# Gate products of one-hot matrices: two products in a rounded format instead of one in plain fp32

## The chip, the cores and the metric

The kernel runs on one core of a Trainium2 chip. A core has a matrix engine (PE), whose weight loads the profile lists apart (PEld), and three engines for element-wise work: VectorE (DVE), ScalarE (ACT) and GpSimd (POOL). SyncE (SP) issues the transfers from the memory outside. Every engine works through its own queue in the order in which its instructions were written there; engines wait for each other by semaphores. The metric is the time of one execution in microseconds (us) on the device.

## The reference

The program is two small networks, one after the other, on 256 tokens of width 1024. The part that matters here is the retrieval of experts (`peer`) in the first. For each token and each of 8 heads it takes the 16 best scores against two sets of 128 keys, forms the 16 best pairs, and turns their scores into gates by a softmax. A pair (i1, i2) names one of 128 x 128 experts:

```python
idx = jnp.take_along_axis(cand_i, pos, axis=-1)          # i1 * 128 + i2
g = jax.nn.softmax(top_s, axis=-1)
act = jax.nn.gelu(jnp.einsum('thkd,td->thk', expert_u[idx], t).astype(jnp.float32))
return jnp.einsum('thk,thkd->td', (g * act).astype(t.dtype), expert_v[idx])
```

So each token has 8 x 16 = 128 slots, each with two indices and a gate. All arithmetic is fp32 in the reference.

## The kernel before

The kernel gathers nothing. It computes the activations of all 128 x 128 experts for all tokens, in a tile X of 128 partitions (i1) x 128 (i2) x 256 tokens, and multiplies them by a matrix of gates that is zero where a token did not choose an expert.

The weights of the whole program come as a stream of 128 x 1024 fp32 tiles ("raw", 4 buffers). Each is split into a high part in the rounded format ("wh": ACT copies it, L296) and a rest ("wl": DVE subtracts, L297), with 3 buffers each, because a product of fp32 accuracy is made of three products of rounded operands (high by high, low by high, high by low: L334 to L336). The rounded format is called fp32r in the profile; plain fp32 operands need no split. The stream is kept three tiles ahead: the split for step i2+3 is written as soon as the buffer of step i2 is free.

The gate stretch is the second part of the loop over i2 (128 steps), which makes the activations of the experts (., i2). A step has 24 products of 128 x 256 on PE into a tile "main". From step 56 on, 64 "gate groups" of four tokens are spread over 70 steps (64 of them hold one group, 6 none). A group makes, per token:

- "oh1" on POOL (L1138): in row "slot", a one where the column number equals the slot's first index;
- "oh2" on DVE (L1141): the same for the second index, times the slot's gate;
- one plain fp32 product oh1 by oh2 on PE (L1144) of 128 x 128 into a tile "aux", which is the token's gate matrix.

The tile's columns of later steps are copied into X by ACT (L1146); the steps already done are multiplied into X by DVE (L1147). Later steps' activations come through a small tile "ge" (gelu on ACT: L1203 for tokens without gates yet, straight into X; L1206 for the others) and are multiplied into X by DVE (L1207). oh1 and oh2 have 4 buffers each, so both are made some groups ahead.

A scheduler in the framework writes the order of every queue at build time. `slots` runs once for each half of the tokens just before the stretch: it transposes the slots' indices and gates, so that a token is a column, into slotT[0] to slotT[2].

Of the kernel before, what the change touches and what calls it, by code (L numbers as in the profile page):

```python
# [8 lines left out]
F32 = mybir.dt.float32  # L9
F32R = mybir.dt.float32r  # L10
U32 = mybir.dt.uint32
U8 = mybir.dt.uint8
AF = mybir.ActivationFunctionType
OP = mybir.AluOpType
# [29 lines left out]
OHB = 4  # L44
# [131 lines left out]
def build(tc, A, out):  # L176
    nc = tc.nc
    V, S, T, G = nc.vector, nc.scalar, nc.tensor, nc.gpsimd

    with ExitStack() as ctx:  # L180
# [8 lines left out]
        def PS():  # L189
            return psum.tile([128, 512], F32, tag="aux", name="aux")  # L190
# [7 lines left out]
        for name in W_IN_ORDER:  # L198
            n = W_IN_COLS[name][1]
# [118 lines left out]
        ident, iota, pair_rows = cst[:, 0:128], cst[:, 128:256], cst[:, 256:272]  # L318
# [141 lines left out]
        with ExitStack() as fctx:  # L460
# [77 lines left out]
            for e in range(2):  # L538
                c = slice(256 * e, 256 * e + 256)
# [116 lines left out]
            def colmajor(ap):  # L656
                return ap.rearrange("p (r w) -> p w r", w=64)
# [290 lines left out]
            def gate_ev(gain):  # L948
                def ev(f, ps):
                    if not gate:  # L950
# [8 lines left out]
                              for g in range(2)], gl_gen(), fm_gen(512, ev, 0, 1),  # L959
                            fm_gen(256, lambda f, ps: S.activation(out=gq[:, f, :].rearrange("p (w r) -> p w r", r=4),  # L960
                                                                   in_=colmajor(ps[:, 0:256]), func=AF.Copy, scale=0.125), 0, 2),
# [35 lines left out]
            for k in st1.end(eps1[:, 0:1], [xlat[:, k] for k in range(8)]):  # L997
                n, o, g, b = xlat[:, k], x1[:, k], vc("lng")[:, k:k + 1], bcen[:, k:k + 1]
# [8 lines left out]
            m2, r = tl("m2", [256], "b0"), tl("r2m", [256], "b1")  # L1007
# [4 lines left out]
            for k in range(8):  # L1012
                n = xlat[:, k]
# [4 lines left out]
                t = tl("tmod", [256], "Qt", 2)  # L1018
# [5 lines left out]
        with ExitStack() as ectx:  # L1024
# [4 lines left out]
            up = uctx.enter_context(tc.tile_pool(name="uphase", bufs=1))  # L1029
# [3 lines left out]
            def carve(shape, dt=F32):  # L1033
                n = int(np.prod(shape))
                o = carve_at[0]
                carve_at[0] += n
                assert carve_at[0] <= 128 * 256
                ap = flat[:, o:o + n]
                if dt is not F32:
                    ap = ap.bitcast(dt)  # L1040
                names = " ".join("abcd"[:len(shape)])
                return ap.rearrange(f"p ({names}) -> p {names}", **dict(zip("abcd", shape))) if len(shape) > 1 else ap
# [13 lines left out]
            tmp2 = carve([256])  # L1056
# [8 lines left out]
            e2 = carve([2, 8, 16])  # L1065
            ii2 = [[carve([8, 16]) for _ in range(2)] + [e2[:, t]] for t in range(2)]
            sm = carve([2, 8])
            slotT = [up.tile([128, 256], F32, name=f"slotT{j}") for j in range(3)]
            qT = [carve([256]) for _ in range(2)]

            def topk16(vals, idx, src, tmp):
# [53 lines left out]
            def slots(t, ii):  # L1125
                pt = PS()
                for j in range(3):
                    T.transpose(pt[:, 128 * j:128 * j + 128], ii[j].rearrange("p h k -> p (h k)"), ident)
                for j in range(3):
                    V.tensor_copy(slotT[j][:, 128 * t:128 * t + 128], pt[:, 128 * j:128 * j + 128])  # L1130

            def gate_group(tg, m):

                t0 = 4 * tg
                oh1 = up.tile([128, 4, 128], F32, name="oh1", tag="oh1", bufs=OHB)
                oh2 = up.tile([128, 4, 128], F32, name="oh2", tag="oh2", bufs=OHB)
                for j in range(4):
                    G.tensor_scalar(oh1[:, j], iota, slotT[0][:, t0 + j:t0 + j + 1], None, op0=OP.is_equal)  # L1138
                pg = PS()
                for j in range(4):  # L1140
                    V.tensor_scalar(oh2[:, j], iota, slotT[1][:, t0 + j:t0 + j + 1], slotT[2][:, t0 + j:t0 + j + 1],  # L1141
                                    op0=OP.is_equal, op1=OP.mult)
                for j in range(4):
                    T.matmul(pg[:, 128 * j:128 * j + 128], oh1[:, j], oh2[:, j], start=True, stop=True)  # L1144
                pgv = pg.rearrange("p (t i) -> p i t", t=4)
                S.activation(out=X[:, m:, t0:t0 + 4], in_=pgv[:, m:], func=AF.Copy)  # L1146
                V.tensor_tensor(X[:, 0:m, t0:t0 + 4], X[:, 0:m, t0:t0 + 4], pgv[:, 0:m], OP.mult)  # L1147
# [32 lines left out]
            for i2 in range(128):  # L1180
                hi, lo = W.get("s")
                p = PM()[:, 0:256]
                for k in range(8):
                    c = slice(128 * k, 128 * k + 128)
# [3 lines left out]
                if i2 < GATE_FROM:  # L1188
                    S.activation(out=X[:, i2, :], in_=p, func=GE)
                    credit += TOPK_RATE  # L1190
                    while (credit > 0 or i2 == GATE_FROM - 1) and not done_tk:
                        try:
                            credit -= next(tk)
                        except StopIteration:
                            done_tk = True
                    if i2 == GATE_FROM - 1:
                        slots(0, ii2[0])
                        slots(1, ii2[1])
                    continue

                t = 4 * done
# [7 lines left out]
                while done < upto:  # L1209
                    gate_group(done, i2 + 1)  # L1210
                    done += 1
# [45 lines left out]
            for i2 in range(125):  # L1257
                w = W.get("s")
                xsplit(i2 + 2)
                x = xs_t.pop(i2)  # L1260
# [530 lines left out]
```

## Time and profile before

| | us |
|---|---|
| median of 3 runs (least, most) | 2248.65 (2248.22, 2250.47) |
| the profiled execution's own time | 2249.63 |
| its span in the profile | 2247.6 |
| gate stretch, 541 to 792 us: PE busy | 251.00 |
| the same: DVE, POOL, ACT busy | 200.55, 207.12, 107.26 |

The span is from the first to the last profiled instruction. A busy time is the union of an engine's instructions. PE and the weight loads overlap, and products overlap each other, so one product's duration is longer than the distance from its start to that of the next; the distance is what a stream of them costs. The same holds, in a smaller measure, for ACT and DVE: an instruction starts a little before the one ahead of it ends. In a waits row, "A line <- B line" says that A sat idle until B's instruction.

### The profile page before, as it was taken

Reading aid. Unit: us, or ns where it says so; the run is one execution under the profiler, and the core shown is the slowest. Engines: PE = TensorE matmul, PEld = TensorE weight load, DVE = VectorE, ACT = ScalarE, POOL = GpSimd, SP = SyncE. Lnnn points to the kernel's source line nnn. Section 1 sums busy time; section 2 is a strip of 40 time slices with the busy share of each in tenths; the row PEclk is TensorE's granted clock in tenths of the full one; section 3 lists DMA queues with packets and bytes.
Section 4 is the critical chain, followed back from the end, with each engine's and each line's share of the span. In section 5 each row is a group of like instructions: output and inputs, shape, how many; then the busy total and the mean of one; then the engine's idle time right before and its main releaser. Section 6 shows DMA issues by size and latency. Waiting matters only on the chain.

```text
span 2247.6 us, 40177 instructions
## 1 busy us (share of the span) xinstructions
PE 2167.5 (96%) x15660; PEld 2034.8 (91%) x15660; DVE 1546.6 (69%) x2819; ACT 1174.9 (52%) x2036; POOL 391.6 (17%) x411
## 2 busy tenths in 40 slices
PE   7999889899999999999989998999999999899998
PEld 4988789899999988888879998899999999889998
DVE  6899879935778866666665556885566555878554
ACT  5755554444444354554554445675456444676443
POOL 0000031225978700000020003020001001302000
PEclk9999899999999999999999999999999999999999
DMA  7544244465444467666646563345564556334564
GB/s 278 160 160 132 85 124 151 160 193 173 143 147 145 141 210 246 197 192 195 202 151 187 171 189 112 100 135 174 174 189 145 173 171 195 103 104 138 185 181 126
DMA packets 101998, 367.37 MB, mean 163 GB/s; under 512 B 11440, under 2 KB 13360, under 8 KB 100528
## 3 DMA queue, kind: packets, MB, share of 16 engines
q1 hardware_dynamic: 101808, 364.81, 51.2%
q8 instruction: 122, 2.00, 0.4%
q14 instruction: 68, 0.56, 0.1%
HBM read 363.72 MB, written 1.05 MB: 162 GB/s over the span
## 4 chain that ended last, share of the span: by engine, by line
PE 79%; DVE 14%; ACT 3%; issue 3%; DMA 1%; POOL 1%; SPq 0%; DVEq 0%; POOLq 0%; ACTq 0%
PE main L336 19%; PE main L335 18%; PE main L334 18%; PE aux L1255 5%; PE aux L1254 5%; PE aux L1256 5%; DVE wl L297 3%; PE aux L1144 3%; DMA raw<-wa 1%; DVE X L1076 1%; DVE X L1074 1%; DVE SB L840 1%; DVE Qt L820 1%; DVE X L1073 0%; DVE X L1075 0%
## 5 line engine op out<-in xcount | busy, mean ns | idle before, releaser
L296 ACT ACTIVATE wh<-raw 128x1024 fp32r<-128x1024 f32 (+1 forms) x630 | 658.2, 1046 | 679.3 <-PE main L335 354.9
L297 DVE TENSOR_TENSOR wl<-raw,wh 128x1024 fp32r<-128x1024 f32 (+1 forms) x606 | 741.0, 1224 | 382.4 <-ACT wh L296 381.9
L336 PE MATMUL main<-hh,wl 128*128 128x256 f32 (+1 forms) x2808 | 807.0, 288 | 17.5 <-DVE wl L297 17.5
L334 PE MATMUL main<-hh,wh 128*128 128x256 f32 (+1 forms) x2808 | 811.8, 290 | 11.5 <-DVE hh L444 5.7
L335 PE MATMUL main<-hl,wh 128*128 128x256 f32 (+1 forms) x2808 | 805.4, 287 | 1.6 <-DVE hl L448 1.1
L336 PEld LDWEIGHTS main<-hh,wl 128*128 128x128 f32 x2808 | 535.2, 191 | 22.0 <-DVE wl L297 20.9
L334 PEld LDWEIGHTS main<-hh,wh 128*128 128x128 f32 x2808 | 534.1, 190 | 16.2 <-DVE hh L444 6.6
L335 PEld LDWEIGHTS main<-hl,wh 128*128 128x128 f32 x2808 | 533.8, 190 | 3.5 <-DVE hl L448 2.2
L396 POOL TENSOR_TENSOR acc<-acc,sqk 128x272 f32<-128x272 f32 (+1 forms) x29 | 37.3, 1286 | 1438.0 <-ACT sqk L389 1437.9
L1138 POOL TENSOR_SCALAR oh<-cst,slotT 128x128 f32<-128x128 f32 x256 | 209.3, 834 | 38.2 <-PE aux L1144 32.4
L334 PE MATMUL main<-ah,wh 128*128 128x272 f32 (+1 forms) x704 | 201.7, 286 | 0.0
L335 PE MATMUL main<-al,wh 128*128 128x272 f32 (+1 forms) x704 | 201.2, 286 | 0.0
L336 PE MATMUL main<-ah,wl 128*128 128x272 f32 (+1 forms) x704 | 200.6, 285 | 0.0
L1254 PE MATMUL aux<-wh,xsh 128*128 128x512 f32 x512 | 199.3, 390 | 0.0
L1255 PE MATMUL aux<-wl,xsh 128*128 128x512 f32 x512 | 199.3, 389 | 0.0
L1256 PE MATMUL aux<-wh,xsl 128*128 128x512 f32 x512 | 199.2, 389 | 0.0
L339 ACT ACTIVATE xsh<-X 128x256 fp32r<-128x256 f32 x128 | 53.4, 418 | 165.7 <-PE aux L1255 163.9
L336 PEld LDWEIGHTS main<-ah,wl 128*128 128x128 f32 x704 | 132.4, 188 | 0.0
L334 PEld LDWEIGHTS main<-ah,wh 128*128 128x128 f32 x704 | 132.3, 188 | 0.0
L335 PEld LDWEIGHTS main<-al,wh 128*128 128x128 f32 x704 | 132.2, 188 | 0.0
L1255 PEld LDWEIGHTS aux<-wl,xsh 128*128 128x128 f32 x512 | 96.1, 188 | 20.2 <-DVE wl L297 0.3
L1254 PEld LDWEIGHTS aux<-wh,xsh 128*128 128x128 f32 x512 | 96.0, 188 | 20.2 <-ACT wh L296 0.3
(507 smaller groups left out, 3126.7 us busy)
## 6 DMA issues: line engine op xcount, KB each, us to landing
raw<-uT SPq DMA_DIRECT2D x128, 512.0 KB, 3.6
raw<-pv SPq DMA_DIRECT2D x128, 512.0 KB, 4.2
raw<-ffn_gate SPq DMA_DIRECT2D x88, 512.0 KB, 3.6
raw<-ffn_up SPq DMA_DIRECT2D x88, 512.0 KB, 3.6
raw<-win SPq DMA_DIRECT2D x72, 512.0 KB, 4.0
raw<-ffn_down SPq DMA_DIRECT2D x64, 512.0 KB, 3.6
raw<-wa SPq DMA_DIRECT2D x32, 512.0 KB, 4.4
raw<-wout SPq DMA_DIRECT2D x24, 512.0 KB, 3.6
```

Source lines behind the costliest of these rows:

```text
L296: S.activation(out=hi[:, :n], in_=t[:, :n], func=AF.Copy)
L297: (G if mode == "p" else V).tensor_tensor(lo[:, :n], t[:, :n], hi[:, :n].bitcast(F32), OP.subtract)
L334: T.matmul(o, lh, rh, start=start, stop=False)
L335: T.matmul(o, lh, rl, start=False, stop=False)
L336: T.matmul(o, ll, rh, start=False, stop=stop)
L339: S.activation(out=hi, in_=src, func=AF.Copy)
L396: (G if self.k < (5 if self.pe == 7 else 2) else V).tensor_tensor(self.acc2, self.acc2, q, OP.add)
L1138: G.tensor_scalar(oh1[:, j], iota, slotT[0][:, t0 + j:t0 + j + 1], None, op0=OP.is_equal)
L1144: T.matmul(pg[:, 128 * j:128 * j + 128], oh1[:, j], oh2[:, j], start=True, stop=True)
L1254: T.matmul(y, x[0][:, c], w[0][:, f], start=(i2 == 0), stop=False)
L1255: T.matmul(y, x[0][:, c], w[1][:, f], start=False, stop=False)
L1256: T.matmul(y, x[1][:, c], w[0][:, f], start=False, stop=(i2 == 127))
```

## The change

Each gate is split into its rounded part and a rest. `slots` stores the rounded gates in slotT[2] (written by ACT in the rounded format, read back as fp32 under the name `rounded`) and in slotT[3] the ratio of the rest to the rounded part: a subtraction, a maximum with 1e-30, a reciprocal and a multiplication on DVE, for each half of the tokens.

In a group, oh1 and oh2 are written in the rounded format, oh2 with the rounded gate. A third tile, oh3, is oh2 times the slot's ratio, made by ACT, four instructions per group. PE makes two products per token, oh1 by oh2 and oh1 by oh3, added up in the same tile. The buffers of the one-hots go from 4 to 3 each.

```diff
-            slotT = [up.tile([128, 256], F32, name=f"slotT{j}") for j in range(3)]
+            slotT = [up.tile([128, 256], F32R if j == 2 else F32, name=f"slotT{j}") for j in range(4)]
+            rounded = slotT[2].bitcast(F32)
...
-                for j in range(3):
-                    V.tensor_copy(slotT[j][:, 128 * t:128 * t + 128], pt[:, 128 * j:128 * j + 128])
+                c = slice(128 * t, 128 * t + 128)
+                for j in range(2):
+                    V.tensor_copy(slotT[j][:, c], pt[:, 128 * j:128 * j + 128])
+                S.activation(out=slotT[2][:, c], in_=pt[:, 256:384], func=AF.Copy)
+                r = rounded[:, c]
+                V.tensor_tensor(slotT[3][:, c], pt[:, 256:384], r, OP.subtract)
+                rec = tmp2[:, 0:128]
+                V.tensor_scalar(rec, r, 1.0e-30, None, op0=OP.max)
+                V.reciprocal(out=rec, in_=rec)
+                V.tensor_tensor(slotT[3][:, c], slotT[3][:, c], rec, OP.mult)
...
-                oh1 = up.tile([128, 4, 128], F32, name="oh1", tag="oh1", bufs=OHB)
-                oh2 = up.tile([128, 4, 128], F32, name="oh2", tag="oh2", bufs=OHB)
+                oh1, oh2, oh3 = [up.tile([128, 4, 128], F32R, name=n, tag=n, bufs=3) for n in ("oh1", "oh2", "oh3")]
...
-                    V.tensor_scalar(oh2[:, j], iota, slotT[1][:, t0 + j:t0 + j + 1], slotT[2][:, t0 + j:t0 + j + 1],
+                    V.tensor_scalar(oh2[:, j], iota, slotT[1][:, t0 + j:t0 + j + 1], rounded[:, t0 + j:t0 + j + 1],
                                     op0=OP.is_equal, op1=OP.mult)
                 for j in range(4):
-                    T.matmul(pg[:, 128 * j:128 * j + 128], oh1[:, j], oh2[:, j], start=True, stop=True)
+                    S.activation(out=oh3[:, j], in_=oh2[:, j].bitcast(F32), func=AF.Copy, scale=slotT[3][:, t0 + j:t0 + j + 1])
+                for j in range(4):
+                    for x in (oh2, oh3):
+                        T.matmul(pg[:, 128 * j:128 * j + 128], oh1[:, j], x[:, j], start=(x is oh2), stop=(x is oh3))
```

The scheduler writes the queues anew. In the rows below a name's number tells the buffer's allocation: wh and wl with neighbouring numbers belong to one weight tile, oh2 and oh3 with neighbouring numbers to one group. Lines after the change: oh2 is L1150, oh3 L1153, the copy of "aux" L1158, its multiplication L1159, the gelus L1215 and L1218, the multiplication by "ge" L1219.

ACT's queue in the middle of the stretch, before the change, two steps:

```order
L1206 ACTIVATE ge_8122<-main_8096 128x184
L1146 ACTIVATE X_2900<-aux_8131 128x21x4
L296 ACTIVATE wh_8194<-raw_8146 128x1024
L1203 ACTIVATE X_2900<-main_8148 128x68
L1206 ACTIVATE ge_8174<-main_8148 128x188
L1146 ACTIVATE X_2900<-aux_8183 128x20x4
L296 ACTIVATE wh_8246<-raw_8198 128x1024
```

ACT's queue after the change, at the same step:

```order
L1158 ACTIVATE X_2900<-aux_8555 128x21x4
L1153 ACTIVATE oh3_8733<-oh2_8732,slotT3_2915 128x128 x4
L296 ACTIVATE wh_8635<-raw_8578 128x1024
L1215 ACTIVATE X_2900<-main_8580 128x68
L1218 ACTIVATE ge_8606<-main_8580 128x188
L1158 ACTIVATE X_2900<-aux_8616 128x20x4
L1153 ACTIVATE oh3_8794<-oh2_8793,slotT3_2915 128x128 x4
L296 ACTIVATE wh_8696<-raw_8639 128x1024
```

The four instructions of oh3 stand right ahead of the copy wh, and each reads an oh2.

DVE's queue at that step, before the change:

```order
L1147 TENSOR_TENSOR X_2900<-X_2900,aux_8131 128x107x4
L1141 TENSOR_SCALAR oh2_8334<-cst_72,slotT1_2913,slotT2_2914 128x128 x3
L1141 TENSOR_SCALAR oh2_8386<-cst_72,slotT1_2913,slotT2_2914 128x128
L297 TENSOR_TENSOR wl_8195<-raw_8146,wh_8194 128x1024
L1207 TENSOR_TENSOR X_2900<-X_2900,ge_8174 128x188
L1147 TENSOR_TENSOR X_2900<-X_2900,aux_8183 128x108x4
L1141 TENSOR_SCALAR oh2_8386<-cst_72,slotT1_2913,slotT2_2914 128x128 x3
L1141 TENSOR_SCALAR oh2_8438<-cst_72,slotT1_2913,slotT2_2914 128x128
L297 TENSOR_TENSOR wl_8247<-raw_8198,wh_8246 128x1024
```

DVE's queue after the change:

```order
L1159 TENSOR_TENSOR X_2900<-X_2900,aux_8555 128x107x4
L1150 TENSOR_SCALAR oh2_8732<-cst_72,slotT1_2913,slotT2_2914 128x128 x4
L297 TENSOR_TENSOR wl_8636<-raw_8578,wh_8635 128x1024
L1219 TENSOR_TENSOR X_2900<-X_2900,ge_8606 128x188
L1159 TENSOR_TENSOR X_2900<-X_2900,aux_8616 128x108x4
L1150 TENSOR_SCALAR oh2_8793<-cst_72,slotT1_2913,slotT2_2914 128x128 x4
L297 TENSOR_TENSOR wl_8697<-raw_8639,wh_8696 128x1024
```

All four oh2 of a group stand ahead of the subtraction wl, which reads the wh that ACT makes behind that group's oh3. PE's queue has, in both kernels, a group's products between the 24 of one step and the 24 of the next: 4 in plain fp32 before, 8 in the rounded format after. The 6 steps without a group lie alike.

## Rows read from the trace of the kernel before

**Rows 1.** The page, part 1, whole span: busy us, share, count of each engine.

```profile
PE 2167.5 (96%) x15660; PEld 2034.8 (91%) x15660; DVE 1546.6 (69%) x2819; ACT 1174.9 (52%) x2036; POOL 391.6 (17%) x411
```

**Rows 2.** Busy time of each engine in the gate stretch (first line names the columns).

```profile
core 0: us, PE busy (x) PEld busy (x) DVE busy (x) ACT busy (x) POOL busy (x), PEclk, DMA share, GB/s
541.00:792.00 251.00, 251.00 (x2151) 250.97 (x2150) 200.55 (x454) 107.26 (x268) 207.12 (x254) 1.00 0.46 145
```

**Rows 3.** Waits in that stretch: who for whom, us in total, times, longest.

```profile
ACT wh L296 <- PE main L335: 145.4, 69, 2.3
DVE oh L1141 <- PE aux L1144: 41.5, 57, 1.4
POOL oh L1138 <- PE aux L1144: 32.4, 49, 3.3
```

**Rows 4.** Timeline of PE, one step: start us, duration us, engine, line, op, tiles, shapes, count.

```profile
644.26 1.05 PE L1144 MATMUL aux<-oh,oh 128*128 128x128 f32 x8
...
645.27 0.28 PE L335 MATMUL main<-hl,wh 128*128 128x256 f32 x1
645.39 0.28 PE L336 MATMUL main<-hh,wl 128*128 128x256 f32 x1
...
648.00 1.05 PE L1144 MATMUL aux<-oh,oh 128*128 128x128 f32 x8
```

**Rows 5.** Timeline of DVE, the same step (idle time and releaser in brackets).

```profile
641.62 0.34 DVE L1141 TENSOR_SCALAR oh<-cst,slotT,slotT 128x128 f32<-128x128 f32 x1 [0.81 <-PE aux L1144]
641.88 1.31 DVE L297 TENSOR_TENSOR wl<-raw,wh 128x1024 fp32r<-128x1024 f32 x1
643.12 0.25 DVE L1207 TENSOR_TENSOR X<-X,ge 128x100 f32<-128x100 f32 x1
643.29 0.49 DVE L1147 TENSOR_TENSOR X<-X,aux 128x336 f32<-128x336 f32 x1
643.71 0.85 DVE L1141 TENSOR_SCALAR oh<-cst,slotT,slotT 128x128 f32<-128x128 f32 x3
```

**Rows 6.** Timeline of ACT, the same step.

```profile
640.61 1.06 ACT L296 ACTIVATE wh<-raw 128x1024 fp32r<-128x1024 f32 x1 [2.13 <-PE main L335]
641.57 0.28 ACT L1203 ACTIVATE X<-main 128x156 f32<-128x156 f32 x1
```

**Rows 7.** Groups by line in that stretch, DVE: busy us, mean ns of one.

```profile
L1147 DVE TENSOR_TENSOR X<-X,aux 128x228 f32<-128x228 f32 (+62 forms) x63 | 32.6, 517 | 0.0
L1207 DVE TENSOR_TENSOR X<-X,ge 128x4 f32<-128x4 f32 (+33 forms) x67 | 18.8, 280 | 0.0
```

**Rows 8.** POOL groups kept apart by shape, whole span.

```profile
L1138 POOL TENSOR_SCALAR oh<-cst,slotT 128x128 f32<-128x128 f32 x256 | 209.3, 834 | 38.2 <-PE aux L1144 32.4 <-DMA raw<-uT 5.8
L297 POOL TENSOR_TENSOR wl<-raw,wh 128x1024 fp32r<-128x1024 f32 x24 | 64.9, 2705 | 233.2 <-ACT wh L296 232.8 <-DVE acc L395 0.3
```

**Rows 9.** ACT groups kept apart by shape, whole span.

```profile
L339 ACT ACTIVATE ah<-sg 128x272 fp32r<-128x272 f32 x66 | 27.4, 414 | 0.9 <-DVE sg L1413 0.9
...
L1333 ACT ACTIVATE gh<-hA,vec 128x272 fp32r<-128x272 f32 x24 | 12.2, 508 | 0.0
...
L1203 ACT ACTIVATE X<-main 128x128 f32<-128x128 f32 x2 | 0.5, 260 | 0.0
...
L1299 ACT ACTIVATE hA<-metaT,nbm 128x128 f32<-128x128 f32 x1 | 0.4, 401 | 1.9 <-PE main L1284 1.9
```

**Rows 10.** Line 1228, ACT: duration ns least, median, most.

```profile
L1228 ACT ACTIVATE hh<-metaT x1: 310/310/310, 801.7 to 801.7; 128x128 fp32r<-128x128 f32 x1
```

**Rows 11.** Timeline of ACT late in the stretch, where DVE waits for it.

```profile
783.53 1.06 ACT L296 ACTIVATE wh<-raw 128x1024 fp32r<-128x1024 f32 x1 [2.26 <-PE main L335]
```

**Rows 12.** Timeline of DVE at that place.

```profile
784.62 1.23 DVE L297 TENSOR_TENSOR wl<-raw,wh 128x1024 fp32r<-128x1024 f32 x1 [1.61 <-ACT wh L296]
```

**Rows 13.** Timeline of the weight loads near the start, two-column products.

```profile
18.71 1.04 PEld L528 LDWEIGHTS aux<-sum,row 128*128 128x128 f32 x8
```

**Rows 14.** Line 1121, DVE: a reciprocal of 16 columns.

```profile
L1121 DVE RECIPROCAL X<-X x1: 237/237/237, 451.0 to 451.0; 128x16 f32<-128x16 f32 x1
```

## The prediction

> **What bounds the kernel now.** I read the page's totals first, then the busy times of the one stretch that the change touches, then who waits there, then one step engine by engine. PE is busy for 2167.5 of 2247.6 us [rows 1]. In the gate stretch (541 to 792 us) it is busy without a gap, at the full clock of 2.4 GHz, while DVE works 200.55, POOL 207.12 and ACT 107.26 of 251 us [rows 2]. The waits agree: ACT idles 145.4 us for buffers that PE frees, DVE 41.5 and POOL 32.4 us for PE to finish with a one-hot buffer [rows 3]. Nobody waits long for anybody but PE. So PE sets the pace, at 3.73 us from one group's products to the next (644.26 to 648.00 [rows 4]). Of these, 24 main products at 0.12 apart (645.27 to 645.39) are 2.84 us; the group's four plain fp32 products, recorded as eight passes, take the other 0.89, 0.111 each.
>
> **Does PE gain?** The trace has no rounded product of 128 columns, so I bound it. Low: a rounded product of 256 columns comes every 0.118 us; 128 columns fewer at 2.4 GHz are 0.053 less, so 0.065 each and 0.52 a group. High: the format is not faster at this width and each of the eight costs what a plain product does, 0.222, so 1.78 a group. Between them stands the weight load: each product loads its 128 columns anew, and eight loads with products of only two columns behind them took 1.04 us from first start to last end [rows 13], (1.04 - 0.19) / 7 = 0.12 apart, 0.19 being the length of one load; so the load, not the product, sets that rate, and it is the rate of the fp32 passes too. I take 0.111, so 0.89 a group: no gain and no loss.
>
> The Trainium skill speaks for a gain: "TensorE: Matmul & The Clock Gate", section "Back-to-back issue gap", gives about 81 ns for a load and product at 128 columns; eight would be an estimated 0.65 us a group and 64 groups 15 us less. The same page's "LDWEIGHTS (loading the stationary operand)" gives columns / 1.2 ns, 107 for 128 columns, which says no gain; the two-column products agree with that one.
>
> **What the change adds.** Per group: four oh3 on ACT. A copy of 128 x 128 with constant operands took 0.260 us (from PSUM) and 0.310 (into the rounded format, from SBUF); 128 x 128 with one per-partition operand 0.401 [rows 9, 10]. At 272 columns the difference between a copy and an instruction with a per-partition scale is 0.508 - 0.414 = 0.094 [rows 9], and 0.310 + 0.094 gives 0.404, so I take 0.40. Low end 0.26, high end 0.508, since 128 columns won't take longer than 272. ACT starts the next instruction 0.10 before the end of the one before (641.57 against 640.61 + 1.06 [rows 6]), so four cost 4 x 0.305 = 1.22 us. By load this is harmless: 64 x 1.22 = 78 us on an engine idle for 144.
>
> The place is what costs. In the new queues oh3 stands ahead of the weight copy wh on ACT, and waits for the group's oh2 on DVE; on DVE the subtraction wl stands behind these oh2 and waits for that wh; and the next group's oh2 stand behind wl and two multiplications into X. That is a closed ring through two queues. It has to be walked once per group, and having buffers does not shorten it. Before, no instruction of ACT waited for oh2, so there was no ring. Its length, from one group's first oh2 to the next one's:
>
> - oh2 until ACT can begin: 0.34, and 0.03 for the semaphore (783.53 + 1.06 to 784.62 [rows 11, 12]); the other three oh2 start 0.26 apart and stay ahead of ACT;
> - four oh3: 1.22;
> - wh 1.06, semaphore 0.03 [rows 11, 12];
> - wl until the next start, 641.88 to 643.12 [rows 5]: 1.24;
> - multiplication by ge: mean 0.280 less the overlap of 0.08 (0.25 against 643.12 to 643.29): 0.20; by aux: 0.517 - 0.08 = 0.44 [rows 5, 7].
>
> Sum 4.56 us, against PE's 3.73. What is late next is wl, and so PE's products L336 with it. Against the trace's own step the ring adds 0.83.
>
> The stretch: groups 5 to 64 walk the ring, 60 x 0.83 = 50 us (the first ones fill empty buffers). A step without a group lies between groups five times; PE needs 2.84 for it, the ring only the extra wl and ge, 1.24 + 0.20 = 1.44, so 5 x 1.40 = 7 us come back. And wl has a lead that is used up first: the wl made at 641.88 is ready at 643.19 and serves the step after the group at 648.00, that is from 648.8 on [rows 4, 5], so 5.6 us. Sum: 50 - 7 - 6 = +37 us.
>
> The rest I cost at nothing. POOL's oh1 (4 x 0.834 = 3.34 a group [rows 8]) has 4.56 us now; writing the rounded format could cost 0.30 more each before POOL decides, and POOL's rounding subtraction of 1024 columns takes 2.705 [rows 8], 0.34 for 128, so the format is no dearer by itself. If POOL did decide, each 0.1 us above that would cost 64 x 0.4 = 26 us. Three buffers in place of four: a group's buffer comes free when its products end and is needed three ring turns later, 13.7 us, for 3.34 of POOL; with the ring gone the 11.2 us of three PE steps still cover it. oh2 in the new format: DVE's multiplications of 100 and 336 columns, 0.25 and 0.49 [rows 5], bound it; only its first of four counts in the ring, so -0.09 to +0.15, -5 to +9 us. `slots`: for each half one copy moves from DVE to ACT and four small DVE instructions come, 0.34 each like oh2, the reciprocal between 0.24 and eight times that [rows 14]: some 2 x 1.3 us, up to 6, once, beside PE's main products; the lead of 5.6 covers it, and where the ring eats that lead, 1 to 6 us return. I leave them to the range.
>
> The profiled execution took 2249.63 us, 2.0 more than its span; 2249.6 + 37 = 2286.6. The median is 1.0 lower, so I say 2286.
>
> **Rivals.**
> 1. The rounded products are as slow as plain ones (0.222 each). For it: 256 columns are the least width that the trace shows in this format. PE's step would be 2.84 + 1.78 = 4.62, just above the ring: 64 x 0.89 = 57 us, 2306. Against it: one rounded product of 256 columns needs 0.118, half of it for 128 if nothing else ties it.
> 2. oh3 is short (0.26). Then four starts are 0.16 apart but can't outrun oh2's 0.26, so three of these and one oh3 count, 0.94 in place of 1.22 and 4.28 in all; with wl at the 1.23 that it has beside an idle POOL [rows 12] (1.15 to the next start) it is 4.19: 60 x 0.46 = 28, less 13, +15 us, 2264. For no change the ring would have to fall to 3.95; that needs oh2 shorter too (0.25, starts 0.17 apart: 4.19 - 0.09 - 0.27 = 3.83), which gives 60 x 0.10 - 13, below zero: the lead covers all, 2250. Against it: the rows with per-partition operands.
> 3. Faster: the ring does not hold PE, because DVE and ACT turn out quick enough for the step, and the eight products run at 0.065. PE gets 0.37 a group, 64 x 0.37 = 24 us: 2226. It decides from a ring below 3.73 - 0.37 = 3.36, so 1.2 us under my sum, all four oh3 gone from it. At rates between, any ring above 3.73 makes PE's saving worth nothing. By the Trainium skill's 81 ns ("TensorE: Matmul & The Clock Gate", "Back-to-back issue gap") this rival would bring 15 us. Against it: wh's 1.06 and wl's 1.24 are measured and in the ring whatever the rest costs.
>
> **How the numbers follow.** Ring as summed 0.71, its own range 2260 to 2300 (oh3 0.31 with quick oh2 to 0.45); rival 1 0.13; oh3 at its high end, with a ring of 4.56 + 4 x 0.107 = 4.99 and 2249.6 + 60 x 1.26 - 13 = 2312, 0.03; rival 2 at no change 0.07; rival 3 0.06. The range of 2258 to 2310 takes in the first two and leaves some 0.16 out. About 0.2% (4.5 us) is what a measurement can tell: faster 0.06, same 0.07, slower 0.87.
>
> **What would show it.** Right: in the gate stretch PE's products L336 (or the gate products) wait for DVE, PE has gaps of about 0.8 us a step, DVE idles for ACT's wh about 1.6 us a step and ACT for oh2; the distance between groups is 4.3 early and 4.8 late, growing as the multiplications widen; eight product records 0.11 apart; the rest of the span unmoved. Wrong: PE gapless with a longer step (rival 1), PE gapless with the old step (rival 2), groups closer than 3.73 (rival 3), or waits for POOL's oh1.

## The result and the profile after

| | median us (least, most; runs) | ratio to before on the same chip, 95% interval |
|---|---|---|
| before | 2249.56 (2248.22, 2250.65; 4) | |
| after | 2282.34 (2280.16, 2285.03; 4) | 1.0147 [1.0135, 1.016] |

The change makes the kernel 32.8 us slower; 2286 was forecast, in a range of 2258 to 2310. The profiled span grew from 2247.6 to 2281.2 us, by 33.6. Where it grew is seen by the same instructions in both traces: the transposes of `slots` just ahead of the stretch, the third group and the last group. PE before:

```profile
537.87 0.82 PE L1128 MATMUL aux<-cst,X 128*128 128x128 f32 x6
548.98 1.05 PE L1144 MATMUL aux<-oh,oh 128*128 128x128 f32 x8
790.92 1.05 PE L1144 MATMUL aux<-oh,oh 128*128 128x128 f32 x8
```

PE after (the last group starts at 825.14 us, in a row further down):

```profile
541.64 0.82 PE L1130 MATMUL aux<-cst,X 128*128 128x128 f32 x6
554.32 1.00 PE L1156 MATMUL aux<-oh,oh 128*128 128x128 f32 x8
```

They start 3.8, 5.3 and 34.2 us later than before, and one more wait of 0.9 us stands right behind the last group. So the ring of the prediction can have cost 28.9 + 0.9 = 29.8 us, from the third group on; 1.6 went between `slots` and the third group. Ahead of the stretch 3.8 us were lost and behind it 1.6 came back. In the experiments below the transposes start between 0.9 us earlier and 4.3 us later than before, whether the stretch loses time or not, so these 2.2 us are not put down to the ring; what makes them stays open.

The page's first part of the kernel after answers to [rows 1]: busy us, share of the span, count.

```profile
PE 2178.5 (95%) x15660; PEld 2035.5 (89%) x15660; DVE 1545.9 (68%) x2825; ACT 1249.4 (55%) x2294; POOL 373.8 (16%) x411
```

ACT has 74 us more work and DVE as much as before, and neither tells anything: both have room to spare. The gate stretch does. Busy times there up to just ahead of the last group, after, with the columns of [rows 2]:

```profile
541.00:824.00 283.00, 263.69 (x2164) 254.80 (x2163) 195.75 (x461) 179.15 (x516) 190.16 (x256) 1.00 0.41 127
```

PE was busy without a gap in [rows 2] and now is for 263.69 of 283 us, at the same full clock. Who waits for whom in that stretch, after (us in total, times, longest), to be held against [rows 3]:

```profile
ACT oh L1153 <- DVE oh L1150: 100.6, 66, 2.2
DVE wl L297 <- ACT wh L296: 87.6, 60, 1.6
POOL oh L1147 <- PE aux L1156: 81.2, 53, 6.2
PEld main L336 <- DVE wl L297: 25.0, 35, 1.0
PE main L336 <- DVE wl L297: 17.8, 33, 0.8
```

Before, everybody waited for PE. Now ACT waits for DVE, DVE for ACT and PE for DVE: a ring, with PE hanging on it. POOL still waits for PE, so POOL is not the cause. The ring can be walked in the rows. DVE after, two turns (start us, duration us):

```profile
661.74 1.23 DVE L297 TENSOR_TENSOR wl<-raw,wh 128x1024 fp32r<-128x1024 f32 x1 [1.46 <-ACT wh L296]
662.89 0.26 DVE L1219 TENSOR_TENSOR X<-X,ge 128x104 f32<-128x104 f32 x1
663.06 0.50 DVE L1159 TENSOR_TENSOR X<-X,aux 128x340 f32<-128x340 f32 x1
663.48 1.17 DVE L1150 TENSOR_SCALAR oh<-cst,slotT,slotT 128x128 fp32r<-128x128 f32 x4
666.12 1.23 DVE L297 TENSOR_TENSOR wl<-raw,wh 128x1024 fp32r<-128x1024 f32 x1 [1.47 <-ACT wh L296]
```

ACT after, beside them:

```profile
663.86 1.28 ACT L1153 ACTIVATE oh<-oh,slotT 128x128 fp32r<-128x128 f32 x4 [1.62 <-DVE oh L1150]
665.04 1.04 ACT L296 ACTIVATE wh<-raw 128x1024 fp32r<-128x1024 f32 x1
```

One turn from wl to wl is 661.74 to 666.12, 4.38 us: wl until the next start 1.15, ge 0.17, aux 0.42, oh2 until ACT begins 0.38, four oh3 1.18, wh until wl 1.08. Each of the two engines idles about 1.5 us a turn, always for the other. PE after, the same time and late in the stretch:

```profile
661.55 1.00 PE L1156 MATMUL aux<-oh,oh 128*128 128x128 f32 x8
...
662.57 0.27 PE L335 MATMUL main<-hl,wh 128*128 128x256 f32 x1
663.02 0.38 PE L336 MATMUL main<-hh,wl 128*128 128x256 f32 x1 [0.19 <-DVE wl L297]
...
665.73 1.00 PE L1156 MATMUL aux<-oh,oh 128*128 128x128 f32 x8
...
820.49 1.00 PE L1156 MATMUL aux<-oh,oh 128*128 128x128 f32 x8
...
825.14 1.01 PE L1156 MATMUL aux<-oh,oh 128*128 128x128 f32 x8
```

Groups are 4.18 us apart here and 4.65 late (3.73 before, [rows 4]). On PE not every group is late: until 617 us, and for three or four groups soon after each step without a group, they still come 3.73 apart, about half of them in all, because wl is ahead of PE there. (A wl of a step without a group comes 1.3 to 1.4 us after the one before it.) The ring itself turns at its own pace all the time, as the first and the last distances from wl to wl show. DVE after:

```profile
556.30 1.23 DVE L297 TENSOR_TENSOR wl<-raw,wh 128x1024 fp32r<-128x1024 f32 x1 [0.52 <-ACT wh L296]
560.45 1.29 DVE L297 TENSOR_TENSOR wl<-raw,wh 128x1024 fp32r<-128x1024 f32 x1 [1.45 <-ACT wh L296]
...
821.20 1.23 DVE L297 TENSOR_TENSOR wl<-raw,wh 128x1024 fp32r<-128x1024 f32 x1 [1.53 <-ACT wh L296]
825.87 1.23 DVE L297 TENSOR_TENSOR wl<-raw,wh 128x1024 fp32r<-128x1024 f32 x1 [1.53 <-ACT wh L296]
```

In PE's rows above, the late product is L336, the first that reads wl. Read such a wait by starts: it comes 0.45 after L335 in place of 0.12, so 0.33 were lost, while the bracket says 0.19, because the record of the product before still counts as busy. That is why PE's idle time in the stretch (19.3 us) is less than the 29.8 us lost there.

### The profile page after: what moved, and what is told of

Same layout as the page of the kernel before. It is cut to its first block, busy times and chain, and to the rows that moved or that the text cites. A ratio compares the mean times of both kernels' runs of the same rounds, so it can differ in the third digit from the quotient of the medians.

```text
span 2281.2 us, 40704 instructions
## 1 busy us (share of the span) xinstructions
PE 2178.5 (95%) x15660; PEld 2035.5 (89%) x15660; DVE 1545.9 (68%) x2825; ACT 1249.4 (55%) x2294; POOL 373.8 (16%) x411
## 4 chain that ended last, share of the span: by engine, by line
PE 73%; DVE 16%; ACT 5%; issue 3%; POOL 1%; DMA 1%; DVEq 0%; SPq 0%; POOLq 0%; ACTq 0%
PE main L336 17%; PE main L335 17%; PE main L334 17%; PE aux L1266 5%; PE aux L1267 5%; PE aux L1268 5%; DVE wl L297 4%; PE aux L1156 2%; ACT wh L296 2%; ACT oh L1153 1%; DVE X L1078 1%; DVE X L1076 1%; DVE X L1159 1%; DVE SB L840 1%; DVE Qt L820 0%
## 5 line engine op out<-in xcount | busy, mean ns | idle before, releaser
L336 PE MATMUL main<-hh,wl 128*128 128x256 f32 (+1 forms) x2808 | 809.9, 289 | 38.8 <-DVE wl L297 38.4
L335 PE MATMUL main<-hl,wh 128*128 128x256 f32 (+1 forms) x2808 | 804.1, 287 | 1.2 <-DVE hl L448 1.1
L336 PEld LDWEIGHTS main<-hh,wl 128*128 128x128 f32 x2808 | 534.2, 190 | 51.2 <-DVE wl L297 49.6
L335 PEld LDWEIGHTS main<-hl,wh 128*128 128x128 f32 x2808 | 533.9, 190 | 3.2 <-DVE hl L448 2.2
L1147 POOL TENSOR_SCALAR oh<-cst,slotT 128x128 fp32r<-128x128 f32 x256 | 190.2, 759 | 88.6 <-PE aux L1156 81.2
L335 PE MATMUL main<-al,wh 128*128 128x272 f32 (+1 forms) x704 | 201.3, 286 | 0.0
L336 PE MATMUL main<-ah,wl 128*128 128x272 f32 (+1 forms) x704 | 200.6, 285 | 0.0
L1153 ACT ACTIVATE oh<-oh,slotT 128x128 fp32r<-128x128 f32 x256 | 83.3, 392 | 100.8 <-DVE oh L1150 100.6
L336 PEld LDWEIGHTS main<-ah,wl 128*128 128x128 f32 x704 | 132.4, 188 | 0.0
L335 PEld LDWEIGHTS main<-al,wh 128*128 128x128 f32 x704 | 132.2, 188 | 0.0
```

The lines of the kernel that those rows point to most:

```text
L335: T.matmul(o, lh, rl, start=False, stop=False)
L336: T.matmul(o, ll, rh, start=False, stop=stop)
L1153: S.activation(out=oh3[:, j], in_=oh2[:, j].bitcast(F32), func=AF.Copy, scale=slotT[3][:, t0 + j:t0 + j + 1])
```

## Experiments

The theory: the time is lost in the ring through the two in-order queues, and neither PE's products nor ACT's work nor the buffers as such cost anything. The rivals: the rounded products are slow; ACT or DVE has too much work; three buffers are too few.

**Opening the ring by buffers.** Only the counts of buffers change:

```diff
-                oh1, oh2, oh3 = [up.tile([128, 4, 128], F32R, name=n, tag=n, bufs=3) for n in ("oh1", "oh2", "oh3")]
+                oh1, oh2, oh3 = [up.tile([128, 4, 128], F32R, name=n, tag=n, bufs=b) for n, b in (("oh1", 3), ("oh2", 4), ("oh3", 2))]
```

> The changed kernel with one number per tile altered: oh2 has 4 buffers and oh3 2, in place of 3 and 3. The same instructions run; ACT's queue stays as it is in the middle of the stretch (oh3 ahead of wh), but DVE's oh2 stand one group further ahead, so the ring from oh2 over oh3, wh and wl back to oh2 now spans two groups. Theory (the ring sets the pace): 4.4 us for two groups can't hold PE at 3.73 a group, so PE is gapless again in the gate stretch and the time is 2245 to 2252 us. Rival (ACT's extra work or oh3's place ahead of wh is the price, whatever oh2 does): unchanged, 2280 to 2285. Rival (the eight rounded products are dearer for PE): unchanged too.

Measured: 2251.19 us, ratio 1.0 [0.9991, 1.0009]. The 33 us are gone, with nine one-hot buffers in all, as in the kernel after. The queues say why. After the change, a wl stands behind each group's oh2 whose wh stands behind the same group's oh3 (DVE: oh2_7503, then wl_7407; ACT: oh3_7504, then wh_7406). With the new counts the same oh2_7503 is followed by wl_7346, and oh3_7504 by wh_7467: oh2 is written a step earlier and oh3 a step later, and the loop closes over three groups instead of one (two had been expected, but ACT's queue moved too). Waits from 541 to 795 us of this run:

```profile
ACT wh L296 <- PE main L335: 70.3, 67, 2.3
DVE wl L297 <- ACT wh L296: 46.6, 64, 1.6
POOL oh L1147 <- PE aux L1156: 28.5, 49, 3.2
...
ACT oh L1153 <- DVE oh L1150: 0.8, 2, 0.6
```

ACT waits for PE again and no longer for oh2. DVE still waits 46.6 us for wh, but no row has PE waiting for DVE: PE is first in every chain. On ACT a group's oh3 still stand ahead of a wh, but this wh now waits for PE:

```profile
642.33 1.28 ACT L1153 ACTIVATE oh<-oh,slotT 128x128 fp32r<-128x128 f32 x4
644.57 1.06 ACT L296 ACTIVATE wh<-raw 128x1024 fp32r<-128x1024 f32 x1 [0.96 <-PE main L335]
```

**Opening the ring by order.** Buffers stay 3 each; oh3 is written behind the step's wh (`wh` keeps the copies by step):

```diff
+                with tc.issue_after(W.wh[W.i].ins):
+                    for j in range(4):
-                for j in range(4):
-                    S.activation(out=oh3[:, j], in_=oh2[:, j].bitcast(F32), func=AF.Copy, scale=slotT[3][:, t0 + j:t0 + j + 1])
+                        S.activation(out=oh3[:, j], in_=oh2[:, j].bitcast(F32), func=AF.Copy, scale=slotT[3][:, t0 + j:t0 + j + 1])
```

> The changed kernel with an order constraint alone: a group's four oh3 are queued on ACT behind the weight copy wh that they stood ahead of. Buffers stay at 3. Theory (ring): wh of that step no longer waits for that group's oh2, the ring spans two groups, PE is gapless, 2244 to 2251 us. Rival (ACT's work as such, or PE's products): 2280 to 2285.

Measured: 2252.04 us, 1.0008 [0.9999, 1.0017]. In the queues oh3_7504 now stands behind wh_7406, so the wl that follows oh2_7503 no longer depends on it, and the loop closes over two groups. Every operation of the change is still there, so the loss was the place of four instructions. From the third group to the last PE takes 241.5 us here and in the run with four oh2 buffers, 241.9 before the change and 270.8 after it.

**The same products without oh3.** PE multiplies oh1 by oh2 twice, so the gates come out doubled; ACT makes no oh3:

```diff
-                    S.activation(out=oh3[:, j], in_=oh2[:, j].bitcast(F32), func=AF.Copy, scale=slotT[3][:, t0 + j:t0 + j + 1])
-                for j in range(4):
-                    for x in (oh2, oh3):
-                        T.matmul(pg[:, 128 * j:128 * j + 128], oh1[:, j], x[:, j], start=(x is oh2), stop=(x is oh3))
+                    for x in range(2):
+                        T.matmul(pg[:, 128 * j:128 * j + 128], oh1[:, j], oh2[:, j], start=(x == 0), stop=(x == 1))
```

> The changed kernel without oh3: the second product of each token takes oh2 again, so PE does the same eight rounded products per group, and ACT has no oh3 (the gates come out doubled). Theory: eight products cost PE what four plain ones did (0.89 a group), no ring, 2246 to 2253 us. Rival (rounded products of 128 columns are slow): 2280 or more. If they were at 0.065 each, PE would gain 64 x 0.37 = 24 us: 2226.

Measured: 2252.26 us, 1.0004 [0.9995, 1.0013]. Eight rounded products of 128 columns cost PE what four plain fp32 ones do. PE in this run, two groups 3.73 us apart as in [rows 4]:

```profile
640.57 1.00 PE L1154 MATMUL aux<-oh,oh 128*128 128x128 f32 x8
644.30 1.00 PE L1154 MATMUL aux<-oh,oh 128*128 128x128 f32 x8
```

**oh3 on DVE.** The multiplication moves to the engine that has more work already:

```diff
-                    S.activation(out=oh3[:, j], in_=oh2[:, j].bitcast(F32), func=AF.Copy, scale=slotT[3][:, t0 + j:t0 + j + 1])
+                    V.tensor_scalar(oh3[:, j], oh2[:, j].bitcast(F32), slotT[3][:, t0 + j:t0 + j + 1], None, op0=OP.mult)
```

> The changed kernel with oh3 made by DVE in place of ACT, right behind oh2. The ring through ACT is gone: wh waits for PE alone. DVE gets four more instructions a group, 4 x 0.26, on top of 2.9: about 3.9 us a group against PE's 3.73 and a little slack in the steps without a group. Theory (ring through ACT's queue was the price): 2248 to 2262 us, with DVE nearly full. Rival (PE's products or the buffers): 2280 to 2285.

Measured: 2252.78 us, 1.001 [1.0001, 1.0019]. Busy times of this run from 541 to 795 us, with the columns of [rows 2]:

```profile
541.00:795.00 254.00, 252.47 (x2157) 251.53 (x2156) 249.87 (x717) 107.62 (x270) 214.27 (x252) 1.00 0.44 144
```

DVE is now busy for 249.87 of 254 us, and the kernel still loses at most 0.2%: in this stretch a nearly full queue without a ring did less harm than two queues with a third of their time free and a ring.

**How many buffers, or equal numbers of them?** Two of each in the kernel after (bufs=2), and three instead of four in the kernel before (OHB = 3):

> The changed kernel with 2 buffers instead of 3 for each of oh1, oh2 and oh3, nothing else. Theory (equal counts close the ring, how many there are does not matter): the ring of 4.4 us a group stays as it is, so the time of the changed kernel again, 2282, between 2278 and 2288; ACT's oh3 still wait for DVE's oh2, about 1.6 us a group. Rival (the step from 4 to 3 buffers costs by itself, because one-hots are made too late for PE): a further buffer less costs as much again, 2315 or more, and PE's gate products or POOL's oh1 wait longest.

> The kernel before with 3 buffers instead of 4 for oh1 and oh2; no oh3, plain fp32 products. Theory: with no instruction of ACT in the chain there is no ring, and a group's buffer has three steps of PE, 11 us, to come back: 2249 to 2252, PE without a gap in the gate stretch. Rival (three buffers are what costs): 2270 to 2285, with waits of DVE or POOL for buffers that reach PE.

Measured: 2287.24 us, 1.0168 [1.0151, 1.0185], and 2250.41, 1.0005 [0.9995, 1.0015]. Three buffers without a ring cost nothing; two with it cost little beyond the ring (4.9 us more than three, by medians of two batches whose kernels before agree within 0.1 us, with the intervals of the ratios overlapping). Waits in the stretch with two of each:

```profile
ACT oh L1153 <- DVE oh L1150: 88.7, 54, 2.1
DVE wl L297 <- ACT wh L296: 79.0, 53, 1.5
POOL oh L1147 <- PE aux L1156: 65.0, 53, 3.4
PEld aux L1156 <- ACT oh L1153: 7.9, 34, 0.2
```

The queues close the same ring, 4.50 us a turn on average. What is new is where PE is held: its gate products wait for oh3 (the last row), and the weight loads of L336, which waited 25.0 us for wl in the kernel after, wait 2.4.

**The ring's arithmetic.** One member is shortened and every queue keeps its order: oh3 with a constant scale, which leaves the true rest of the gates out.

```diff
-                    S.activation(out=oh3[:, j], in_=oh2[:, j].bitcast(F32), func=AF.Copy, scale=slotT[3][:, t0 + j:t0 + j + 1])
+                    S.activation(out=oh3[:, j], in_=oh2[:, j].bitcast(F32), func=AF.Copy, scale=2.0 ** -12)
```

> The changed kernel with a constant instead of the slot's ratio as the scale of oh3, so the gates' rest is not the right one; every queue stays in the order of the changed kernel. It shortens one member of the ring and nothing else. Theory: a copy with constant operands took 0.31 us, the four starts come 0.21 apart instead of 0.295, but the last of them can't begin before the fourth oh2 has ended (0.83 + 0.34 + 0.03 us after the first one's start), so wh starts 1.20 + 0.21 = 1.41 us after the first oh2 instead of 1.56: the ring falls by 0.15, 60 x 0.15 = 9 us less, 2273 (2269 to 2277); 4 x 0.09 x 60 = 22 less, 2260, would be the most. Rival (the time is lost elsewhere, or ACT's oh3 is not in the chain): 2282.

Measured: 2273.62 us, 1.0107 [1.0086, 1.0128]: 8.7 us below the kernel after (9 expected), or 0.40% by the ratios. Line L1153 in this run (duration ns least/median/most, first and last start):

```profile
L1153 ACT ACTIVATE oh<-oh x256: 298/311/317, 544.7 to 815.3; 128x128 fp32r<-128x128 f32 x128
```

The same line in the kernel after:

```profile
L1153 ACT ACTIVATE oh<-oh,slotT x256: 384/388/405, 546.5 to 824.5; 128x128 fp32r<-128x128 f32 x128
```

From the first oh3 to the last it is 270.6 us in place of 278.0, so the gain is where the ring is. The wl of this run, to be held against 556.30 and 825.87 above:

```profile
554.70 1.34 DVE L297 TENSOR_TENSOR wl<-raw,wh 128x1024 fp32r<-128x1024 f32 x1 [0.74 <-ACT wh L296]
...
816.64 1.23 DVE L297 TENSOR_TENSOR wl<-raw,wh 128x1024 fp32r<-128x1024 f32 x1 [1.33 <-ACT wh L296]
```

That is 261.9 us in place of 269.6 for the same 59 turns and five extra wl, 0.13 less a turn where 0.15 was expected. The 77 ns less of each oh3 would be 18 us over 60 turns of four; less than half came, since the fourth oh3 can't begin before DVE's fourth oh2 has ended: it starts 0.03 us after that end in each of these 59 groups, where it was 0.06 to 0.26 us in the kernel after. A ring is shortened only by what is its longest way at that place. The Trainium skill ("ScalarE: Activation LUTs", section "What ACT_TABLE_LOAD costs") gives 186 ns plus 0.833 a column with constant operands and some 93 more for a per-partition one, by estimate 293 and 386 here; the medians, 311 and 388, agree within 20.

**What PE could gain.** Only the rounded gates, four products a group, the gates' rest left out:

```diff
-                oh1, oh2, oh3 = [up.tile([128, 4, 128], F32R, name=n, tag=n, bufs=3) for n in ("oh1", "oh2", "oh3")]
+                oh1, oh2 = [up.tile([128, 4, 128], F32R, name=n, tag=n, bufs=3) for n in ("oh1", "oh2")]
...
-                    for x in (oh2, oh3):
-                        T.matmul(pg[:, 128 * j:128 * j + 128], oh1[:, j], x[:, j], start=(x is oh2), stop=(x is oh3))
+                    T.matmul(pg[:, 128 * j:128 * j + 128], oh1[:, j], oh2[:, j], start=True, stop=True)
```

> The changed kernel without oh3 and its products: four products a group, oh1 by oh2 in the rounded format, so the gates' rest is left out. This prices one rounded product of 128 columns and says what the change could bring at most. By 0.111 us each, PE's group falls from 0.89 to 0.44 and its step from 3.73 to 3.28: 64 x 0.44 = 28 us less, 2222; POOL's oh1 at 0.76 each, 3.04 a group, just keeps up, and if it takes 0.83 it sets 3.34 and 2226. By 0.065 each 64 x 0.63 = 40 less by PE, but POOL holds it near 2216 to 2226, PE then waiting for oh1. By 0.222 each: no change, 2250.

Measured: 2221.84 us, 0.9878 [0.9861, 0.9894]. PE in this run:

```profile
639.96 0.56 PE L1153 MATMUL aux<-oh,oh 128*128 128x128 f32 x4
643.24 0.56 PE L1153 MATMUL aux<-oh,oh 128*128 128x128 f32 x4
```

Four products fewer bring 3.73 - 3.28 = 0.45 us a group, 0.11 each, and 64 x 0.45 = 29 us; 28 were measured.

**A version that beats both.** One-hots in bf16, with the gate's bf16 part in oh2 and the rest in oh3, and oh3 behind wh as above:

```diff
-            slotT = [up.tile([128, 256], F32R if j == 2 else F32, name=f"slotT{j}") for j in range(4)]
-            rounded = slotT[2].bitcast(F32)
+            slotT = [up.tile([128, 256], F32, name=f"slotT{j}") for j in range(4)]
+            half = up.tile([128, 256], BF, name="half")
+            rounded = slotT[2]
...
-                S.activation(out=slotT[2][:, c], in_=pt[:, 256:384], func=AF.Copy)
+                S.activation(out=half[:, c], in_=pt[:, 256:384], func=AF.Copy)
+                S.activation(out=slotT[2][:, c], in_=half[:, c], func=AF.Copy)
...
-                oh1, oh2, oh3 = [up.tile([128, 4, 128], F32R, name=n, tag=n, bufs=3) for n in ("oh1", "oh2", "oh3")]
+                oh1, oh2, oh3 = [up.tile([128, 4, 128], BF, name=n, tag=n, bufs=3) for n in ("oh1", "oh2", "oh3")]
```

> The changed kernel with oh1, oh2 and oh3 in bf16 (the gates' rounded part in bf16, the rest as oh3, which leaves a relative error of a gate of some 2 to the minus 17), and with ACT's oh3 behind the copy wh of the same step, as in the run with that order. If the weight load sets the rate whatever the format: eight products at 0.111, 2250 to 2253, no change. If the load of 128 columns in bf16 is shorter: down to 0.065 each, 0.37 a group less, 64 x 0.37 = 24 us less, 2226, as long as POOL's oh1 (0.76 to 0.83 each) keeps up with a step of 3.36.

Measured: 2225.16 us, 0.9894 [0.9877, 0.991], 24 us below the kernel before. PE in this run:

```profile
640.52 0.62 PE L1161 MATMUL aux<-oh,oh 128*128 128x128 bf16 x8
...
643.87 0.62 PE L1161 MATMUL aux<-oh,oh 128*128 128x128 bf16 x8
```

The step is 3.35 us. Less the 2.84 of the main products that is 0.51 for a group of eight, 0.064 each, where rounded and plain ones cost 0.89 and 0.111. The group of the weight loads of the gate products in this run (mean ns is the number before the last bar):

```profile
L1161 PEld LDWEIGHTS <-oh 128*128 128x128 bf16 x512 | 29.4, 98 | 3.5
```

The same group in the kernel after, 541 to 824 us:

```profile
L1156 PEld LDWEIGHTS aux<-oh,oh 128*128 128x128 f32 x504 | 62.3, 191 | 1.0 <-ACT oh L1153 0.5 <-issue 0.2
```

A load of 128 bf16 columns takes 98 ns instead of 191, and the 0.064 are about the 0.065 that the prediction worked out for products which no load holds up. This fits a load that no longer sets the rate; no run changes the load alone. The Trainium skill ("TensorE: Matmul & The Clock Gate", section "Weight-path perf modes — Fast Weight Load (FWL) and DoubleRow") has a faster load for 128 weights of a type other than FP32, about twice as fast; the ratio here is 1.95. POOL's group of oh1 in the bf16 run:

```profile
L1151 POOL TENSOR_SCALAR oh<-cst,slotT 128x128 bf16<-128x128 f32 x256 | 215.0, 858 | 13.5 <-PE aux L1161 7.7 <-DVE slotT L1136 5.8
```

That is 215.0 / 64 = 3.36 us a group, as much as PE's step; POOL keeps up by the steps without a group and has 13.5 us of idle time in the whole stretch. By estimate a faster PE would find POOL in its way.

The last run leaves the order to the scheduler:

> The bf16 kernel without the edit of the order: the scheduler puts oh3 ahead of wh again, but here it also divides a group's oh2 on DVE, two ahead of wl and two behind the multiplications. Theory: the ring still closes, but with one oh2 and one or two oh3 in it instead of all four: 0.34 + 0.03 + 0.295 + 1.04 + 0.03 + 1.15 + 0.20 + 0.44 = 3.52 us against PE's 3.34, and the first divided groups have a lead: 60 x 0.18 = 11 less the lead of 6 to 13, so 2225 to 2232. Rival (any oh3 ahead of wh costs the full ring of 4.4): 2280, PE's gain worth nothing.

Measured: 2227.08 us, 0.99 [0.9882, 0.9918], no different from the version with the edit. The scheduler there divides a group's oh2 around wl. Counted in the order of the records, the loop from wl back to wl closes over one step in 23 of 60 cases and over two or more in the other 37. Waits of this run, 541 to 795 us:

```profile
ACT wh L297 <- PE main L336: 22.8, 28, 1.9
ACT oh L1156 <- DVE oh L1153: 22.5, 24, 1.4
DVE oh L1153 <- PE aux L1159: 15.7, 41, 0.8
```

ACT waits about as long for oh2 as for PE, and no wait of PE for DVE is listed. I had expected a ring of 3.52 against 3.34, with a few us lost; the groups are 3.34 apart. The estimate had the loop close over one step every time. The bf16 products under the full ring were not tried; that a faster PE brings nothing there rests on the waits of the kernel after alone.

## Why the prediction was right, point by point

- **PE gains nothing and loses nothing.** Right: the group's step was 3.73 us in every run with eight rounded products and no ring, and four of them were worth 0.45. That the weight load sets the rate is supported by the bf16 run, where a load of half the length brings the distance from 0.111 to 0.064. Rival 1 (0.222 each) falls with the run of doubled oh2, rival 3's 0.065, and the 0.081 by which it would bring 15 us, with the same.
- **oh3's duration.** 0.40 was taken, 0.388 measured, 0.295 from start to start where 0.305 was taken. Rival 2's short oh3 was not what happened.
- **The ring.** Right in place and mechanism: two changes that only open it, by buffers and by order, give all of the loss back. Its length was 4.38 us in the turn above, 4.46 on average, and 4.56 by the sum. Half of the 0.18 by which that turn is shorter is wl: 1.24 was read beside a busy POOL [rows 5], and 1.15 is what it takes when POOL is idle beside most of it, which [rows 12] had shown (1.23 long); the rest is oh3 (0.04) and the two multiplications (0.05). The forecast distances, 4.3 early and 4.8 late, came out as 4.15 and 4.67 from wl to wl. On PE the forecast of gaps of about 0.8 us in every step did not come true: about half of the groups stay 3.73 apart, and the lateness falls on the others.
- **The sum.** +37 was forecast, +32.8 measured, but the ring alone cost 29.8. The wl rows separate the terms. From 556.30 to 825.87 us DVE makes 59 turns and five extra wl; these five come 1.27 to 1.44 us after the one before, 6.7 in all, which leaves 262.8 us, 4.455 a turn. Against PE's 3.73 that is 59 x 0.725 = 42.8 us, where 60 x 0.83 = 50 was forecast. The five steps without a group give back 5 x 2.84 - 6.7 = 7.5 (forecast 7), and 42.8 - 7.5 - 29.8 leaves a lead of 5.5 (forecast 6). So lead and empty steps were sized rightly, and the mis-sized term is the ring, 4.46 in place of 4.56 us, 7 us too much in all. That the time came out only 4 below the forecast is in part luck: 1.6 us of `slots` and 2.2 from outside the stretch, which the sum has at nothing, made up for about half of it.
- **"Having buffers does not shorten it."** Wrong as a general sentence. It holds for equal numbers (three or two of each give the same ring), but four buffers for oh2 and two for oh3 move the two apart in the queues and spread the loop over several groups. The step failed in taking the new order for given, when it follows from the buffer counts. It did not harm the forecast, since the counts were equal.
- **Three buffers, POOL, slots at nothing.** Right for three buffers by the run of the kernel before with three, and for POOL by its waits for PE (81.2 us in the kernel after, 28.5 with four oh2 buffers). `slots` is not quite nothing: from its transposes to the third group PE takes 12.7 us instead of 11.1, and 12.4 to 12.7 in the runs with four oh2 buffers, with oh3 behind wh and without oh3. These 1.3 to 1.6 us lie in the 1 to 6 that the prediction left to its range; in the runs without a ring they are too little to show in the median.

## What to carry to other kernels

When work is moved to an engine that is "idle enough", write down what its instruction waits for and what stands behind it in the queue; if the path leads back to the queue it came from, the length of that loop, over the number of iterations it spans, is a bound like an engine's load. Here such a loop was opened by order or by giving the producer's tile four buffers and the consumer's two, and then the same work cost nothing that could be measured; all of it on the producer's engine, then 98% busy, cost 0.2% at most. And before splitting a plain fp32 product in two rounded ones at 128 columns, see what the weight load costs in each format: here bf16 halves paid and fp32r halves did not.

## What the runs showed of the hardware

- POOL's and DVE's times go together. Four oh1 of the same form took 2.66 us in the kernel after, where DVE idles beside them for part of the time, and 3.49 in the run with four oh2 buffers, where it works more (one oh1 took 0.759 and 0.864 us on average over the stretch). POOL's timeline, after:

```profile
662.72 2.66 POOL L1147 TENSOR_SCALAR oh<-cst,slotT 128x128 fp32r<-128x128 f32 x4 [1.38 <-PE aux L1156]
```

  And with four oh2 buffers:

```profile
641.94 3.49 POOL L1147 TENSOR_SCALAR oh<-cst,slotT 128x128 fp32r<-128x128 f32 x4 [0.24 <-PE aux L1156]
```

  What the two share, no run here shows. It matters for sums: wl is 1.23 us long on average in the stretch after the change and was 1.28 before, so a ring can be a little shorter than its members' rows from a busier kernel say.
- Eight rounded products of 128 columns cost a step 0.89 us, just as eight passes of plain fp32, and eight bf16 products 0.51, all with a weight load each.
